# Packet sizes and store order in a transfer-bound image rotation: two slabs turned as a pair

## The chip, the cores and the metric

The kernel runs on one core of a Trainium2 chip. The metric is device time in microseconds (us).

## The reference

```python
batch, c, h, w = 32, 3, 256, 256
def reference(x):                       # float32
    return np.rot90(x, k=-1, axes=(-2, -1)).astype(np.float32)
```

96 images of 256 x 256 floats are rotated by 90 degrees. 25.17 MB are read and 25.17 MB written, and nothing is calculated.

## The kernel before

The images are cut into 12 slabs of 2 MB, eight images each. A slab is loaded into a buffer (`unit`), turned by VectorE in two transposes, and stored. All loads stand in the queue ahead of all stores. (In the cuts of code, "..." marks what is left out, and comments in English are added.) Slab n is turned into the place that slab n - 1 has left, so twelve buffers and one in PSUM are enough.

The way in which a slab lies in its buffer sets the size of the contiguous pieces ("packets") that a transfer moves. "Short" means 8 rows, 8 KB; "long" means 16 rows, 16 KB. With these turns, a slab may have long packets on one side only: long in and short out, or short in and long out.

```python
RL, RS = 16, 8
I = 2
long_st = (0, 1, 2, last)               # short loads, long stores; the others the reverse
...
for n in range(n_slabs):
    t_in, t_out = units[n], units[n - 1] if n else turned0
    if n in long_st:
        ...                             # two transposes
    else:
        src = t_in.rearrange("p i f -> p (i f)").rearrange("p (r g c) -> p c r g", r=RL, c=RS)
        dst = t_out.rearrange("p i (c k r) -> p c r k i", c=RS, r=RL)[:, :, ::-1, ::-1, :]
        for h in range(2):
            cs = slice(h * RS // 2, (h + 1) * RS // 2)
            nc.vector.transpose(out=dst[:, cs], in_=src[:, cs])
    if n in range(5, last):
        nc.sync.dma_start(out=st_short[n], in_=t_out)          # one store of 2 MB
    elif n:
        for i in range(I):
            st = store(n, t_out, i)                            # two stores of 1 MB
            ...                         # slab 1's first store is ordered after slab 11's first load
```

Slab 0 is turned into PSUM, copied back to SBUF by ScalarE at the end, and stored last.

## Time and profile before

| | before |
|---|---|
| time, median of the first 3 runs | 123.80 us (123.74 to 123.87) |
| span of the profile | 121.9 us |
| packet time, share of 16 engines' span | 98.1% |
| VectorE busy | 92.9 us (76%) |
| packets | 5248: 3072 of 8 KB, 1536 of 16 KB, 640 tiny ones for semaphores |

The lines on which the argument rests are shown in the prediction below. Two more from the profile's page: the groups of VectorE work (line, engine, operation, names, shapes, count | busy us, mean ns of one | idle time before) and the packet count.

```profile
DMA packets 5248, 50.33 MB, mean 413 GB/s; under 512 B 640, under 2 KB 640, under 8 KB 640
...
L98 DVE STREAM_TRANSPOSE u<-u 128x2048 f32<-128x2048 f32 x16 | 62.4, 3947 | 0.3
L92 DVE STREAM_TRANSPOSE u<-u 128x2048 f32<-128x2048 f32 x6 | 23.4, 3984 | 0.1
```

A transpose of 2048 columns takes 3.95 to 3.98 us, and VectorE waits for nothing in between.

### The profile page before, as it was taken

To read this page: it belongs to the slowest core of one execution; us is meant where nothing else is said; L and a number is where in the kernel's file an instruction comes from. 1 tells how busy PE (TensorE), PEld (TensorE's weight loads), DVE (VectorE), ACT (ScalarE), POOL (GpSimd) and SP (SyncE) were. 2 spreads that over 40 slices of the span, in tenths; PEclk is the share of its full clock that TensorE was granted. 3 is DMA by queue.
4 is the path that set the end of the run, shared out by engine and by line. 5 is a ranking of instruction groups with operands and counts; after the bars stand their busy time and mean duration, and the time that the engine had idled before them with its cause. 6 is when DMAs were issued, how large, how long until landed. Compare 5 with 4: busy or idle time off the path is not lost.

```text
span 121.9 us, 137 instructions
## 1 busy us (share of the span) xinstructions
DVE 92.9 (76%) x24; ACT 4.9 (4%) x3; POOL 0.2 (0%) x4
## 2 busy tenths in 40 slices
DVE  0039999999999999999999999999999992000000
ACT  0000000000000000000400000000000007400000
POOL 0000000000000000000000000000000000000000
DMA  3999999999999999999999999999999999999994
GB/s 86 430 430 430 427 433 430 430 430 430 430 430 430 430 430 430 430 430 390 427 468 430 430 390 430 430 430 430 411 419 419 427 419 419 414 427 473 425 419 188
DMA packets 5248, 50.33 MB, mean 413 GB/s; under 512 B 640, under 2 KB 640, under 8 KB 640
## 3 DMA queue, kind: packets, MB, share of 16 engines
q1 hardware_dynamic: 5248, 50.33, 98.1%
HBM read 25.17 MB, written 25.17 MB: 413 GB/s over the span
## 4 chain that ended last, share of the span: by engine, by line
DVE 44%; issue 29%; DMA 6%; DVEq 3%; ACT 2%; ACTq 1%; SPq 0%
DVE u L98 26%; DVE u L92 12%; DVE turned L92 6%; DMA u<-in_x_dram 6%; DVEq L138 3%; ACT u L110 2%; ACTq L138 1%; SPq L73 0%; DVEq L92 0%
## 5 line engine op out<-in xcount | busy, mean ns | idle before, releaser
L98 DVE STREAM_TRANSPOSE u<-u 128x2048 f32<-128x2048 f32 x16 | 62.4, 3947 | 0.3
L92 DVE STREAM_TRANSPOSE u<-u 128x2048 f32<-128x2048 f32 x6 | 23.4, 3984 | 0.1
L92 DVE STREAM_TRANSPOSE turned<-u 128x2048 f32<-128x2048 f32 x2 | 7.1, 3586 | 8.1 <-DMA u<-in_x_dram 8.1
L110 ACT COPY u<-turned 128x2048 f32<-128x2048 f32 x2 | 3.6, 1869 | 40.5 <-DVE u L92 40.5
L110 ACT ACT_TABLE_LOAD x1 | 1.3, 1283 | 59.6 <-DMA u<-in_x_dram 59.6
L127 POOL MEMSET const-bfloat16-1.0<- 128x1 bf16 x1 | 0.1, 102 | 0.0
L127 POOL MEMSET const-uint8-127<- 128x1 uint8 x1 | 0.1, 102 | 0.0
L127 POOL MEMSET const-float32-0.0<- 128x1 f32 x1 | 0.1, 99 | 0.2 <-issue 0.2
L127 POOL MEMSET const-float32-1.0<- 128x1 f32 x1 | 0.1, 99 | 0.0
## 6 DMA issues: line engine op xcount, KB each, us to landing
u<-in_x_dram SPq DMA_DIRECT2D x20, 1024.0 KB, 19.6
out_dram<-u SPq DMA_DIRECT2D x12, 1024.0 KB, 12.1
out_dram<-u SPq DMA_DIRECT2D x6, 2048.0 KB, 20.9
u<-in_x_dram SPq DMA_DIRECT2D x2, 2048.0 KB, 13.5
```

The costliest lines, as they stand in the source:

```text
L92: nc.vector.transpose(out=dst[:, cs], in_=src[:, cs])
L98: nc.vector.transpose(out=dst[:, cs], in_=src[:, cs])
L110: nc.scalar.copy(out=units[last][:, i], in_=turned0[:, i])
L127: nc = _bacc.Bacc("TRN2", target_bir_lowering=False, num_devices=1)
L138: with _tile.TileContext(nc) as tc:
```

## The change

The intent is to have long packets on more sides. Slabs 8 and 9 are turned together, as a pair: with two neighbouring buffers read as one and two neighbouring buffers written as one, both sides can be long. The place of the pair must be two free, adjacent buffers; these are those of slabs 3 and 7. Buffer 3 holds slab 4's turned data, so slab 4 must be stored before the pair is turned. That is why slab 4 is stored ahead of all; 3 and 5 to 7 follow, and 1 and 2 come behind them. Slab 10 changes from long loads and short stores to the reverse.

```diff
-    long_st = (0, 1, 2, last)
+    long_st = (0, 1, 2, 10, 11)
+    both = (8,)
+    paired = [n + a for n in both for a in range(2)]
...
+    adjacent = [(3, 7), (8, 9)]        # these share one tile
...
+    for n in (0, 1, 2, 3, 7, 4, 5, 6, *range(8, n_slabs)):      # order of the loads
...
+        elif n in paired:
+            src = pairs[both.index(n) + 1].rearrange("p a (r g c) -> p c r g a", r=RL, c=RL)
+            dst = pairs[both.index(n)].rearrange("p i (c k r) -> p c r k i", c=RL, r=RL)[:, :, ::-1, ::-1, :]
+            parts, step = 4, RL // 4
...
+    for n in range(both[0]):
+        turn(n)
+    for n in (4, 3, 5, 6, 7, 1, 2):
+        st = store(n)                  # 3 to 7 as one store of 2 MB each
+    for n in range(both[0], n_slabs):
+        turn(n)
+        store(n)
```

| | loads of 16 KB | loads of 8 KB | stores of 16 KB | stores of 8 KB | order of the stores |
|---|---|---|---|---|---|
| before | 3 to 10 | 0, 1, 2, 11 | 0, 1, 2, 11 | 3 to 10 | 1, 2, 3 ... 11, 0 |
| after | 3 to 9 | 0, 1, 2, 10, 11 | 0, 1, 2, 8 to 11 | 3 to 7 | 4, 3, 5, 6, 7, 1, 2, 8 ... 11, 0 |

More of the change, by code (lines that the diff above doesn't have):

```diff
@@ L60, with fours @@
     ld_short, ld_long, st_short, st_long = short(rows_in), long(rows_in), short(rows_out), long(rows_out)
-    pools = [ctx.enter_context(tc.tile_pool(name=f"unit{u}", bufs=1)) for u in range(n_slabs)]
-    units = [pool.tile([P, I, F], fp32, name=f"u{u}") for u, pool in enumerate(pools)]
-    psum = ctx.enter_context(tc.tile_pool(name="psum", bufs=1, space=bass.MemoryType.PSUM))
-    turned0 = psum.tile([P, I, F], fp32, name="turned0")
-    for n in range(n_slabs):
-        if n in (1, 2):
-            ld = nc.sync.dma_start(out=units[n], in_=ld_short[n])
+    units = [None] * n_slabs
+    adjacent = [(3, 7), (8, 9)]
+    pairs = []
+    for us in adjacent + [(u,) for u in range(n_slabs) if all(u not in us for us in adjacent)]:
+        pool = ctx.enter_context(tc.tile_pool(name=f"unit{us[0]}", bufs=1))
+        held = pool.tile([P, len(us), I * F], fp32, name=f"u{us[0]}")
+        for j, u in enumerate(us):
+            units[u] = held[:, j]
+        pairs.append(held)
+    psum = ctx.enter_context(tc.tile_pool(name="psum", bufs=1, space=bass.MemoryType.PSUM))
+    turned0 = psum.tile([P, I * F], fp32, name="turned0")
+    def fours(t):
+        return t.rearrange("p (i f) -> p i f", i=I)
+    for n in (0, 1, 2, 3, 7, 4, 5, 6, *range(8, n_slabs)):
+        if n in (1, 2, 10):
+            nc.sync.dma_start(out=fours(units[n]), in_=ld_short[n])
             continue
@@ L72 @@
             if n in long_st:
-                ld = nc.sync.dma_start(out=units[n][:, i], in_=ld_short[n][:, i])
+                ld = nc.sync.dma_start(out=fours(units[n])[:, i], in_=ld_short[n][:, i])
             else:
-                ld = nc.sync.dma_start(out=units[n][i::I].rearrange("p i f -> p (i f)"), in_=ld_long[n, i])
+                ld = nc.sync.dma_start(out=units[n][i::I], in_=ld_long[n, i])
             if (n, i) == (last, 0):
                 mark = ld
-    def store(n, t, i):
+    home = [turned0] + units[:last]
@@ L80, in store, with turn @@
+    def turn(n):
         if n in long_st:
-            return nc.sync.dma_start(out=st_long[n, i], in_=t[i::I].rearrange("p i f -> p (i f)"))
-        return nc.sync.dma_start(out=st_short[n][:, i], in_=t[:, i])
-    for n in range(n_slabs):
-        t_in, t_out = units[n], units[n - 1] if n else turned0
-        if n in long_st:
-            src = t_in.rearrange("p i (r g c) -> p c r g i", r=RS, c=RL)
-            dst = t_out.rearrange("p i f -> p (i f)").rearrange("p (c k r) -> p c r k", c=RL, r=RS)[:, :, ::-1, ::-1]
-            pieces = 2
-            for h in range(pieces):
-                cs = slice(h * RL // pieces, (h + 1) * RL // pieces)
-                nc.vector.transpose(out=dst[:, cs], in_=src[:, cs])
-        else:
-            src = t_in.rearrange("p i f -> p (i f)").rearrange("p (r g c) -> p c r g", r=RL, c=RS)
-            dst = t_out.rearrange("p i (c k r) -> p c r k i", c=RS, r=RL)[:, :, ::-1, ::-1, :]
-            for h in range(2):
-                cs = slice(h * RS // 2, (h + 1) * RS // 2)
-                nc.vector.transpose(out=dst[:, cs], in_=src[:, cs])
-        if n in range(5, last):
-            nc.sync.dma_start(out=st_short[n], in_=t_out)
-        elif n:
-            for i in range(I):
-                st = store(n, t_out, i)
-                if (n, i) == (1, 0):
-                    tc.add_manual_dep(st.ins, mark.ins.name, mybir.DependencyInfo(
-                        mybir.DependencyClass.Sync, mybir.DependencyReason.SCHED_ONLY), reason="stores after loads")
@@ new lines, in turn @@
+            src = fours(units[n]).rearrange("p i (r g c) -> p c r g i", r=RS, c=RL)
+            dst = home[n].rearrange("p (c k r) -> p c r k", c=RL, r=RS)[:, :, ::-1, ::-1]
+            parts, step = 2, RL // 2
+        elif n in paired:
+            if n not in both:
+                return
+            src = pairs[both.index(n) + 1].rearrange("p a (r g c) -> p c r g a", r=RL, c=RL)
+            dst = pairs[both.index(n)].rearrange("p i (c k r) -> p c r k i", c=RL, r=RL)[:, :, ::-1, ::-1, :]
+            parts, step = 4, RL // 4
+        else:
+            src = units[n].rearrange("p (r g c) -> p c r g", r=RL, c=RS)
+            dst = fours(home[n]).rearrange("p i (c k r) -> p c r k i", c=RS, r=RL)[:, :, ::-1, ::-1, :]
+            parts, step = 2, RS // 2
@@ new lines, in turn, with store @@
+        for h in range(parts):
+            nc.vector.transpose(out=dst[:, h * step : (h + 1) * step], in_=src[:, h * step : (h + 1) * step])
+    def store(n):
+        if n in paired:
+            first = n if n in both else n - 1
+            for i in range(I):
+                nc.sync.dma_start(out=st_long[n, i], in_=pairs[both.index(first)][n - first :: I, i])
+        elif n in long_st:
+            for i in range(I):
+                nc.sync.dma_start(out=st_long[n, i], in_=home[n][i::I])
+        else:
+            return nc.sync.dma_start(out=st_short[n], in_=fours(home[n]))
@@ L109 @@
+    for n in range(both[0]):
+        turn(n)
+    for n in (4, 3, 5, 6, 7, 1, 2):
+        st = store(n)
+        if n == 4:
+            tc.add_manual_dep(st.ins, mark.ins.name, mybir.DependencyInfo(
+                mybir.DependencyClass.Sync, mybir.DependencyReason.SCHED_ONLY), reason="stores after loads")
+    for n in range(both[0], n_slabs):
+        turn(n)
+        store(n)
     for i in range(I):
-        nc.scalar.copy(out=units[last][:, i], in_=turned0[:, i])
-    for i in range(I):
-        store(0, units[last], i)
+        nc.scalar.copy(out=fours(units[last])[:, i], in_=fours(turned0)[:, i])
@@ L116 @@
+    home[0] = units[last]
+    store(0)
 _INS = ['x']
```

## The prediction

> **What bounds the kernel now.** The program moves 25.17 MB in and 25.17 MB out and only rearranges in between, so I read the slices and the queue line of the page first, to see whether the transfers ever stop.
>
> ```profile
> DVE  0039999999999999999999999999999992000000
> DMA  3999999999999999999999999999999999999994
> GB/s 86 430 430 430 427 433 430 430 430 430 430 430 430 430 430 430 430 430 390 427 468 430 430 390 430 430 430 430 411 419 419 427 419 419 414 427 473 425 419 188
> ...
> q1 hardware_dynamic: 5248, 50.33, 98.1%
> ...
> DVE 44%; issue 29%; DMA 6%; DVEq 3%; ACT 2%; ACTq 1%; SPq 0%
> ```
>
> The row DMA is at 9 from the second slice to the one before the last: the 16 transfer engines are full for the whole run, at 98.1% of the span. The last line here, the chain that ended last, would name VectorE (44%) and "issue" (29%). It is to be distrusted: it follows semaphores back from the last instruction, and the last instruction is the wait for the last store. The row DVE falls to 0 six slices (18 us) before the end, while the transfers go on. VectorE keeps up, with slack; it does not set the end.
>
> The second view is busy time by stretch (start:end, length, busy time of DVE, ACT and POOL, clock, DMA share, GB/s). I cut it where the packet records change size: 8 KB loads, 16 KB loads, 16 KB stores, 8 KB stores, 16 KB stores.
>
> ```profile
> 7.30:17.20 9.90, 9.10 (x3) 0.00 (x0) 0.00 (x0) 1.00 1.00 424
> 17.20:56.30 39.10, 38.93 (x11) 0.00 (x0) 0.00 (x0) 1.00 1.01 429
> 61.30:71.00 9.70, 9.63 (x4) 0.00 (x0) 0.00 (x0) 1.00 1.01 432
> 71.00:110.70 39.70, 30.27 (x8) 3.63 (x2) 0.00 (x0) 1.00 1.01 423
> 110.70:120.50 9.80, 0.00 (x0) 0.00 (x0) 0.00 (x0) 1.00 1.01 428
> ```
>
> Share 1.00 to 1.01 everywhere: no idle transfer engine inside, loads first and then stores, one after the other. The rate is 424 to 432 GB/s whatever the packet size. All that a change of packet sizes can win lies in that small difference.
>
> The third view is the timeline from 54 us and the SyncE queue's waits, for the slack of the engines behind the transfers:
>
> ```profile
> 59.63 3.97 SPq L81 DMA_DIRECT2D out_dram<-u  x4
> 59.64 1.28 ACT L110 ACT_TABLE_LOAD   x1 [59.64 <-DMA u<-in_x_dram]
> ...
> 93.56 7.82 DVE L92 STREAM_TRANSPOSE u<-u 128x2048 f32<-128x2048 f32 x2
> 101.40 5.57 SPq L81 DMA_DIRECT2D out_dram<-u  x4
> ```
> ```profile
> SPq L81 <- DMA u<-in_x_dram: 16.8, 1, 16.8
> SPq L81 <- DVE u L92: 7.4, 1, 7.4
> ```
>
> The first store is issued at 59.63 us, held 16.8 us by the load it is ordered after. Slab 11's stores are issued at 101.40 us, right after its turn; in the packet records they only begin to move at 110.72 us. So VectorE is some 9.3 us ahead of the transfers at the end.
>
> From the packet records, each slab of 2 MB takes (sum of its packets' durations over 16 engines, in us): slab 0's load 5.37 (start-up), 8 KB loads of slabs 1, 2 and 11 4.94, 4.99 and 5.02, 16 KB loads 4.91 each; 16 KB stores 4.89 each at 61 to 71 us and 4.93 each at the end; 8 KB stores 4.95, 4.95, 4.98 and 5.01 for slabs 3 to 6, and 5.02 to 5.05 for 7 to 10. Loads 59.62, stores 59.65, together 119.27. The first packet starts at 1.76 us and the last ends at 120.77 us: that is 119.01 us, the packets overlapping a trifle. The remaining 2.9 us of the span are start-up and the last landing.
>
> **What the Trainium skill says.** "DMA: Bandwidth & Descriptors", section "Where 436 GB/s comes from": 16 ports of 32 bytes at 850 MHz, 435.2 GB/s, are the ceiling. The trace agrees: 423 to 432 GB/s is 97 to 99% of it, so no ordering can win over 3%. The same page, "Why small descriptors are slow (HBM only)": an overhead of about 3 cycles a packet beside one cycle for 32 bytes. An estimate with that page's 850 MHz clock is 3.5 ns a packet. The loads agree: two median 8 KB packets of 309 ns against one of 614 ns (mean) leave 4 ns. The late stores show more, two of 314 ns (means) against 616.6 ns: 11 ns. Measured numbers are used below. "Anatomy of one DMA — SWDGE (gpsimd) path" puts most of its 2.0 us fixed cost in the write receipt; these DMAs are issued from SyncE, not GpSimd, and the trace shows 1.16 us from the last packet's end (120.77) to the end of the span (121.93).
>
> **The change part by part.**
> Loads. Slab 10 goes from 16 KB to 8 KB packets, the other eleven keep their size (slab 7 only comes earlier). Slab 10 costs 5.0 instead of 4.91: +0.08 us. The DMAs stay 40 (22 loads + 18 stores become 21 + 19).
> Stores. Slabs 8, 9 and 10 go from 8 KB to 16 KB: three at 5.02 become three at about 4.93, -0.28 us. The five that stay 8 KB (3 to 7) move to the front, where before the first four cost 4.95 to 5.01: I take 4.97 each, 24.85, against 24.93 for the same slabs before: -0.08. Slabs 1 and 2 move back, where I take 4.91 instead of 4.89: +0.04. Slabs 11 and 0 stay last. Sum of stores -0.32.
> All packets: -0.24 us. A second way agrees: 512 packets of 8 KB become 256 of 16 KB; the overall means, 314.4 and 614.0 ns, save 14.8 ns a pair, 256 x 14.8 / 16 = 0.24 us.
> VectorE. Still 24 transposes of 2048 columns a partition. The pair's four read with a larger step, but the two forms in place now, with quite different steps, take 3947 and 3984 ns a piece, so I keep 3.95 us: no change of the 92.9 us. What moves is when the pair's outputs come free: all four pieces must be done before slab 8 or 9 can be stored, 70.0 + 4 x 3.93 = 85.8 us.
> Waits. The build's order of instructions shows the pair waiting on the store of slab 4, whose place it overwrites; that is why slab 4 is stored first. That store moves at about 61.4 to 66.4 us and has landed at some 67.6 (with the 1.16 us above); VectorE is free for the pair at 70.0 us. Hidden by 2.4 us. In the new order, slab 8's stores have their turn in the transfers at 61.4 + 7 x 4.95 = 96.1 us, 10.3 us after the pair is turned; slab 10's at 106, turned at 93.7; slab 11's at 111, turned at 101.5; slab 0's at 116, copied by ScalarE at 105. Every step stays hidden.
> The sum: 123.8 - 0.24, rounded with the changeover below to 123.6 us.
>
> **The rivals.**
> 1. A bubble at the changeover from loads to stores. The first store is now one DMA of 2 MB (issues of such stores last 1.2 us here, first issues of 1 MB 0.5 us). At the start, 1.03 us pass from the first issue to the first packet; 59.63 + 1.03 = 60.7, before the loads run dry at 61.6. If packets only start after the whole 1.2 us issue, the engines idle a few tenths of a us: 123.8 to 124.0. I put 0.1 us of it into the sum.
> 2. The pair's wait takes over. For it: four pieces in a row with one release, behind a store that has just begun. Against it: a margin of 2.4 us before VectorE waits at all, and then 8 to 10 us before the transfers feel it. It would need pieces of over 6 us: then 127 or so. Little chance.
> 3. The order, not the size, made the late 8 KB stores dear (4.95 rising to 5.05 while slabs go by): then those moved forward cost 4.95 each, or those in the late places all gain more, another -0.2: 123.3. If the drift belongs to the slab and not to the size, the gain shrinks to 0.1: 123.7.
> 4. The 16 KB stores cure more than packet durations show. They cannot: the engines have no idle time for it. Even all 24 slab transfers at 4.89 would save 119.27 - 117.4 = 1.9 us, 1.5%.
>
> **Range and chances.** Every path but 2 stays within half a per cent. Runs of the kernel before spread by 0.13 us. I predict 123.6 us, range 123.0 to 124.1, faster by over 2% 0.02, within 2% 0.96, slower by over 2% 0.02.
>
> **What would show it.** In the profile after: the queue line at about 98% with 4992 packets; the stretch of 16 KB stores at the end at 427 GB/s or above, and 8 KB stores in front; summed packet time near 119.0 us; DVE near 93 us in 24 pieces of 3.9 us without a wait before the pair over 0.5 us; no slice in the middle of the row DMA under 9. It would be wrong if that row has a hole at 61 us (rival 1), if VectorE waits for a store for many us (rival 2), or if packets of one size changed their duration by over 2%.

## The result

The changed kernel takes 123.33 us (median of 6 runs, 123.22 to 123.68) against 123.84 us (123.74 to 123.90). The ratio is 0.9964, 95% interval 0.9950 to 0.9977. Ratios here are the mean time of one kernel's fast runs over that of the other's of the same rounds, so not quite the ratio of the medians that are quoted. Measured twice more, in later rounds, the ratio was 0.9978 (0.9964 to 0.9992) and 0.9971 (0.9958 to 0.9983). The change wins 0.2 to 0.4%: 0.27 to 0.45 us of 123.8.

First, the slices and the queue line of the page after, to be held against those that the prediction shows:

```profile
DVE  0039999999999999999999999999999990000000
DMA  2999999999999999999999999999999999999994
GB/s 78 426 431 421 431 456 431 431 421 421 431 426 431 431 431 426 404 421 415 418 431 431 429 431 429 423 429 429 464 426 426 426 431 431 431 431 426 431 431 194
DMA packets 4992, 50.33 MB, mean 414 GB/s; under 512 B 640, under 2 KB 640, under 8 KB 640
q1 hardware_dynamic: 4992, 50.33, 97.9%
```

The transfers still never stop, the packets are the 4992 that were expected, and the mean rate went from 413 to 414 GB/s. There is no hole in the middle of the row DMA, where the loads give way to the stores.

Second, busy time by stretch (start:end, length, busy time of DVE, ACT and POOL with counts, clock, DMA share, GB/s), cut where the packet size changes: 8 KB loads, 16 KB loads, 8 KB loads, 8 KB stores, 16 KB stores.

```profile
7.40:17.20 9.80, 8.99 (x3) 0.00 (x0) 0.00 (x0) 1.00 1.01 425
17.20:51.50 34.30, 34.16 (x10) 0.00 (x0) 0.00 (x0) 1.00 1.01 429
51.50:61.40 9.90, 9.87 (x3) 1.28 (x1) 0.00 (x0) 1.00 1.00 419
61.50:86.00 24.50, 24.40 (x8) 0.00 (x0) 0.00 (x0) 1.00 1.01 429
86.00:120.10 34.10, 14.20 (x4) 3.63 (x2) 0.00 (x0) 1.00 1.01 429
```

The stretch of 8 KB stores is the one to look at. Before it ran at 423 GB/s (71.00 to 110.70 us, in the prediction). Now it runs at 429, as fast as 16 KB packets. Where a stretch is cut shifts such a rate by a few GB/s, so this is a hint and no more; the table below has the times.

Third, VectorE after, in the groups of the page and in the timeline (start us, us, engine, line, operation, names, count).

```profile
L116 DVE STREAM_TRANSPOSE u<-u 128x2048 f32<-128x2048 f32 x22 | 84.6, 3912 | 0.3
```
```profile
15.29 84.94 DVE L116 STREAM_TRANSPOSE u<-u 128x2048 f32<-128x2048 f32 x22
...
84.56 4.76 SPq L122 DMA_DIRECT2D out_dram<-u  x4
92.41 13.42 SPq L125 DMA_DIRECT2D out_dram<-u  x6
```

The 22 transposes follow one another from 15.29 us with 0.3 us of idle time in sum: VectorE didn't wait for the pair's place. The pair was done at 84.56 us, when its stores were issued; in the packet records they begin to move at 95.68 us, 11.1 us later. The pair stays hidden.

The gain is too small for whole views, so I take it from the packet records, slab by slab. There are two measures. One is the prediction's: durations of a slab's packets, summed over 16 engines. The other is by the clock: the mean end of a slab's last 16 packets less that of the slab before. Packet records overlap a little, so the second is 0.02 to 0.05 us smaller for most slabs, and only the second adds up to the time that passed.

| stretch (us) | predicted change | summed durations, before to after | by the clock, before to after |
|---|---|---|---|
| load of slab 0 (with the start-up) | 0 | 5.37 to 5.18 | 7.46 to 7.56 |
| load of slab 10 | +0.08 | 4.91 to 5.02 | 4.89 to 4.97 |
| the other ten loads | 0 | 49.33 to 49.32 | 49.07 to 49.06 |
| stores of 3 to 7 (8 KB, moved to the front) | -0.08 | 24.93 to 24.73 | 24.72 to 24.51 |
| stores of 8 to 10 (8 KB to 16 KB) | -0.28 | 15.07 to 14.71 | 14.93 to 14.65 |
| stores of 1 and 2 (moved back) | +0.04 | 9.78 to 9.78 | 9.74 to 9.74 |
| stores of 11 and 0 | 0 | 9.87 to 9.82 | 9.83 to 9.79 |

By the clock the stores win 0.54 us (59.23 to 58.69), and the loads lose 0.17, of which 0.08 is slab 10. The rest, 0.10 in slab 0's load, is start-up; it was 7.48 and 7.45 us in the other two profiles of the same kernel, so it is chance. The last packet ends at 120.37 us instead of 120.77.

The records show one thing more. A packet that nothing disturbs takes 309 ns (8 KB) or 611 ns (16 KB), to the nanosecond. In the profile before, the 8 KB stores ran so until 79 us; from there to the end most took 312 to 319 ns. After the change, hardly one packet between 63 and 93 us is longer than that floor.

### The profile page after: what moved, and what is told of

Same layout as the page of the kernel before. It is cut to its first block, busy times and chain, and to the rows that moved or that the text cites. A ratio compares the mean times of both kernels' runs of the same rounds, so it can differ in the third digit from the quotient of the medians.

```text
span 121.5 us, 135 instructions
## 1 busy us (share of the span) xinstructions
DVE 91.7 (75%) x24; ACT 4.9 (4%) x3; POOL 0.2 (0%) x4
## 2 busy tenths in 40 slices
DMA packets 4992, 50.33 MB, mean 414 GB/s; under 512 B 640, under 2 KB 640, under 8 KB 640
## 3 DMA queue, kind: packets, MB, share of 16 engines
q1 hardware_dynamic: 4992, 50.33, 97.9%
## 4 chain that ended last, share of the span: by engine, by line
DVE 56%; issue 17%; DMA 6%; DVEq 3%; ACT 2%; ACTq 1%; SPq 0%
DVE u L116 50%; DVE turned L116 6%; DMA u<-in_x_dram 6%; DVEq L169 3%; ACT u L141 2%; ACTq L169 1%; SPq L92 0%; DVEq L116 0%
## 5 line engine op out<-in xcount | busy, mean ns | idle before, releaser
L116 DVE STREAM_TRANSPOSE u<-u 128x2048 f32<-128x2048 f32 x22 | 84.6, 3912 | 0.3
```

The source lines that it names most:

```text
L116: nc.vector.transpose(out=dst[:, h * step : (h + 1) * step], in_=src[:, h * step : (h + 1) * step])
```

## The experiments

Two theories. **P:** the gain is the packet sizes: fewer packets, each with its fixed cost. **O:** a good part is the order: the five slabs that stay at 8 KB are stored in an undisturbed stretch, where 8 KB packets are nearly as good as 16 KB ones. Each run below gave the right output.

**after_again: the changed kernel once more.** No edit.

> The changed kernel once more, on this chip, as the mark for the other three. Both theories: about 123.3 us, ratio to before 0.996. Its packet times should again show clean stretches (8 KB stores at 309 ns, 16 KB at 611 ns) in the front part of the stores. If the late point at which packets get longer (93.8 us in the first profile) moves about from run to run, that point is chance and part of the gain is luck; if it stays, something in the program sets it.

Measured: 123.51 us (123.31 to 123.71), ratio 0.9978. The profile has the same clean front; this time packets get longer from 78 us on, not from 94. So when the disturbance starts moves about in this kernel, while the floor stays. By the mark set above, that point is chance, and a small part of the first profile's gain is luck: by the clock the stores take 58.69, 58.74 and, in after_third, 58.77 us.

**order_only: the sizes of before in the order of after.**

```diff
+    for n in (4, 3, 5, 6, 7, 1, 2, 8, 9, 10, last):
+        ...                     # two long stores of 1 MB, or one short one of 2 MB
```

> Packet sizes, loads and buffers of before; only the order of the stores is that of the change (4, 3, 5, 6, 7, 1, 2, then 8, 9, 10, 11, 0), 5248 packets. Theory P (the gain is the 256 saved packets alone): nothing gained, 123.8 us, ratio 1.000. Theory O (the gain is largely that the 8 KB stores come in a stretch where packets run undisturbed): slabs 3 to 7 take 24.73 us instead of 24.93, so 123.6 us, ratio 0.998; slabs 8 to 10 stay at 5.02 each. If both act, O's number here and about 123.5 in size_only.

The edit does one thing more: slabs 3 and 4 go out as one store of 2 MB each, as in the change, where the kernel before has two of 1 MB. So there are 5216 packets, not 5248.

Measured: 123.71 us (123.61 to 124.00), ratio 0.9995 (0.9982 to 1.0007): no difference that the runs can tell. The profile shows what the order does. The stretches are 8 KB stores (3 to 7), 16 KB stores (1, 2), 8 KB stores (8 to 10); the last, of 16 KB stores, is left out:

```profile
61.30:85.80 24.50, 24.40 (x7) 0.00 (x0) 0.00 (x0) 1.00 1.01 429
85.80:95.50 9.70, 9.63 (x4) 0.00 (x0) 0.00 (x0) 1.00 1.00 428
95.50:110.45 14.95, 6.04 (x2) 3.63 (x2) 0.00 (x0) 1.00 1.01 421
```

Slabs 3 to 7 run at 429 GB/s and take 24.53 us, as in the change. Slabs 8 to 10, still 8 KB, run at 421 GB/s and take 14.88 us. The profiled run was also the quickest of the five, 123.61 us. So O's effect is visible in one profile (0.19 us in slabs 3 to 7), but the order alone is not shown to make the kernel faster.

**size_only: the sizes and the pair of after, with slabs 1 and 2 stored first again.**

```diff
-    for n in (4, 3, 5, 6, 7, 1, 2):
+    for n in (1, 2, 4, 3, 5, 6, 7):
```

> Pair, packet sizes and loads of the change, 4992 packets; the stores of slabs 1 and 2 come first again, as before (1, 2, 4, 3, 5, 6, 7, then 8 to 11, 0). Theory P: slabs 8 to 10 take 14.71 us instead of 15.07 and everything else is as in the change, 123.3 to 123.4 us, ratio 0.996 to 0.997. Theory O: most of the gain is lost, 123.6 to 123.8. VectorE should now wait some 7 us before the pair, since slab 4's store lands at about 77.3 us instead of 67.6; the pair is done at about 92 us and its stores have their turn at 96, so that wait should cost nothing.

Measured: 123.45 us (123.36 to 123.47), ratio 0.9967 (0.9955 to 0.9980), beside 0.9978 of the change in the same rounds. The gain stays without the new place of slabs 1 and 2. By the stretches (16 KB stores, 8 KB stores, 16 KB stores) and the wait:

```profile
61.40:71.10 9.70, 8.72 (x3) 0.00 (x0) 0.00 (x0) 1.00 1.02 437
71.10:95.70 24.60, 18.58 (x6) 0.00 (x0) 0.00 (x0) 1.00 1.01 426
95.70:119.90 24.20, 11.45 (x3) 3.63 (x2) 0.00 (x0) 1.00 1.02 434
```
```profile
DVE u L116 <- issue: 6.9, 1, 6.9
```

Cuts at slab borders shift these rates by a few GB/s, so I use the records: the 8 KB stores of slabs 3 to 7, now from 71 to 96 us, still take 24.52 us, and almost no packet is longer than its floor up to the end. Theory O said that a late place makes 8 KB packets dear. It falls: the same places that cost up to 5.00 us a slab before cost 4.90 to 4.92 here. But P does not account for the whole gain either. By the clock the stores of 8 to 10, whose packets grew, win 0.34 us here (14.93 to 14.59), and those of 3 to 7, whose packets did not, win 0.20 (24.72 to 24.52). VectorE waited 6.9 us for the pair's place (the view names no releaser; slab 4's last packet ended at 76.45 us, and VectorE started at 77.08). It cost nothing, as worked out.

**unpaired: slabs 8 and 9 treated as 10 and 11 are, without the pair.**

```diff
-    long_st = (0, 1, 2, 10, 11)
-    both = (8,)
+    long_st = (0, 1, 2, 8, 9, 10, 11)
+    both = ()
```

> The change without its pair: slabs 8 and 9 are loaded in 8 KB packets and turned one by one, as 10 and 11 are; all stores as in the change. 5248 packets less 128 x 2 on the store side and more on the load side. Theory P: two 8 KB loads at 5.02 us instead of 4.91, 0.2 us above the change, 123.5 us. If the pair in itself costs or wins by when it releases its stores: a difference other than 0.1 to 0.3.

Measured: 123.60 us (123.51 to 123.96), ratio 0.9985 (0.9972 to 0.9997), against 0.9978 of the change beside it. The loads of slabs 8 to 11 run at

```profile
41.40:61.40 20.00, 19.93 (x6) 1.28 (x1) 0.00 (x0) 1.00 1.00 417
```

where the change, with 16 KB loads for 8 and 9, has

```profile
41.70:61.40 19.70, 19.63 (x6) 1.28 (x1) 0.00 (x0) 1.00 1.01 424
```

The two loads cost 9.94 us instead of 9.79 by the clock. The pair is worth these 0.15 us in the profile. The times, 0.09 us apart, cannot settle it: their intervals overlap.

Held against order_only, this run gives the cleanest test of P: the order of the stores and the number of packets (5216) are the same, and slabs 8 to 10 are stored in packets of 16 KB instead of 8 (with loads and turns to match). By the clock those three stores take 14.66 us instead of 14.88, and slabs 3 to 7 take 24.56 and 24.53. What is won on the stores is lost again on the loads of 8 to 10, now short. The other profiles agree: slabs 8 to 10 take 14.88 to 14.95 us in the four where they are stored in 8 KB packets, and 14.59 to 14.70 in the eight with 16 KB packets and no gap.

**half_packets: the kernel before, with the stores of slabs 5 to 10 in 4 KB packets.**

```diff
-            nc.sync.dma_start(out=st_short[n], in_=t_out)
+            for k in range(2):
+                ks = slice(k * F // 2, (k + 1) * F // 2)
+                nc.sync.dma_start(out=st_short[n][:, :, ks], in_=t_out[:, :, ks])
```

> The kernel before with the stores of slabs 5 to 10 in 4 KB packets instead of 8 KB (two column halves for each, 1536 packets more, 6784 in all). If a packet costs the 3.5 ns[...] (and that the undisturbed stretches show: 4.90 against 4.87 us a slab for 128 packets more), 1536 x 3.5 / 16 = 0.34 us more: 124.2 us. If it costs the 11 ns that the late stores of before showed, 1.06 us more: 124.9 us.

Measured: 125.72 us (125.68 to 125.81), ratio 1.0158 (1.0142 to 1.0173), slower by 2.0 us: more than either number expected. (The packets are 6880, not the 6784 that I had counted: six more stores bring 96 tiny semaphore packets.) The stretch of slabs 3 and 4, left at 8 KB, and that of the 4 KB stores:

```profile
71.00:80.80 9.80, 9.77 (x3) 0.00 (x0) 0.00 (x0) 1.00 1.01 425
80.80:112.00 31.20, 20.57 (x6) 3.63 (x2) 0.00 (x0) 1.00 1.02 398
```

The six slabs take 31.61 us instead of 29.83 by the clock. 1.78 us x 16 engines over 1536 more packets is 18.5 ns for each packet more. In the records the undisturbed floor of a 4 KB packet is 159 ns, and two of them make 318 ns, 9 ns more than one of 8 KB; their mean is 167.5 ns. So smaller packets do cost time, and in a disturbed stretch a packet costs more than at its floor. That is P, with a cost that is not constant.

**pair_late: slab 4 stored last of the seven.**

```diff
-    for n in (4, 3, 5, 6, 7, 1, 2):
+    for n in (3, 5, 6, 7, 1, 2, 4):
```

> The change, but slab 4, whose store frees the pair's place, is stored last of the seven (3, 5, 6, 7, 1, 2, 4). Sizes and counts are the same, so a theory of packet sizes alone says 123.5 us. The reading of the waits says: slab 4's store lands at about 97 us instead of 67.6, VectorE then needs 14.7 us for the pair's four pieces, slab 8's stores begin at about 113 us instead of 95.7, the transfer engines idle for 17 us, and the time is 140 to 142 us. This is rival 2 of the prediction made to happen.

Measured: 140.78 us (two runs), ratio 1.1374 (1.1353 to 1.1395). From the slices, the wait and the stretch of the gap:

```profile
DVE  0069999999999999999910000001999999994000
...
DMA  4999999999999999999999999995000079998995
```
```profile
DVE u L116 <- DMA out_dram<-u: 26.5, 1, 26.5
```
```profile
96.00:112.20 16.20, 15.47 (x5) 0.00 (x0) 0.00 (x0) 1.00 0.00 0
```

VectorE waits 26.5 us for the store of slab 4, and then the transfers stand still for 16.2 us while the pair is turned. This is rival 2 of the prediction made to happen. Same packets, same sizes, 14% slower: the place of slab 4 in the order is what keeps the pair's wait hidden; it is not what wins the 0.3%.

**before_again: the kernel before, profiled a second time.** No edit.

> The kernel before, for a second profile. In the first one, the 8 KB stores ran at 309 ns up to 79 us and then, from about 1 us after a 2 MB store was issued at 77.9 us, at 312 to 316 ns to the end; larger disturbances followed the issues at 85.7 and 93.6 us. If the program sets this, the second profile shows the same three places; if it is chance, they lie elsewhere. Time 123.8 us either way.

Measured: 123.93 us. Packets held up by 45 to 58 ns lie at 79, 87 and 95 us again, about 1 us after the stores issued at 78.0, 85.8 and 93.7 us; a further one lies at 72 to 74 us. The excess over the floor, summed over the packets of one microsecond, is 94, 421 and 650 ns at 79, 87 and 94 us in the first profile, and 283, 563 and 437 ns in the second, where the next microsecond has 602 ns. So in this kernel the places come back, and something in the program has a part in where packets are held up.

**split_stores: the stores of slabs 5 to 10 as two of 1 MB, against the suspicion that the 2 MB issues disturb.**

```diff
-        if n in range(5, last):
+        if n in range(5, 5):
```

> The kernel before with the stores of slabs 5 to 10 as two DMAs of 1 MB each, as those of 3 and 4 already are, instead of one of 2 MB; packets stay 8 KB, the order stays. Both profiles of before show packets held up by 30 to 58 ns about 1 us after the 2 MB stores issued at 77.9, 85.8 and 93.6 us, and longer packets from then on. Theory H (those 2 MB issues set the disturbance, and the change gains partly because its late stores are 1 MB): slabs 5 to 10 fall from 4.93 to 5.01 us by the clock of the packets to about 4.91, some 0.3 us less, 123.5 us. If the disturbance has another cause: 123.8 us, as before, and slabs 7 to 10 stay near 4.98.

Measured: 123.90 us, ratio 1.0017 (1.0004 to 1.0029). Slabs 8 to 10 take 14.95 us by the clock, as before. Theory H falls. Only the size of the issues is ruled out, though, not the issues as such. In after_third, too, the excess has peaks (53, 126 and 175 ns summed over one microsecond, at 85, 93 and 101 us) about 1 us after stores are issued (84.66, 92.51 and 100.36 us); but size_only issues stores at 91.50, 99.36 and 107.21 us and shows none. So an issue alone is not enough.

A rival stands untested. Slabs 3 to 7 take 24.72, 24.81 and 24.75 us in the three profiles with the order of before, and 24.51 to 24.56 in all ten with any of the changed orders, order_only among them. All ten also store slabs 3 and 4 as one store of 2 MB each instead of two of 1 MB, and no run tests that alone. What sets the disturbance, and why the stores after the change meet less of it, stays open.

**two_pairs, two_pairs_again, two_pairs_long_first: the change carried on.** Slabs 10 and 11 become a second pair, turned into the place of 8 and 9; the third of these kernels also stores 1 and 2 directly behind 4.

```diff
-    long_st = (0, 1, 2, 10, 11)
-    both = (8,)
-    adjacent = [(3, 7), (8, 9)]
+    long_st = (0, 1, 2)
+    both = (8, 10)
+    adjacent = [(3, 7), (8, 9), (10, 11)]
```

> The change carried on: slabs 10 and 11 become a second pair, turned into the place that slabs 8 and 9 left, so that all loads but those of slabs 0 to 2 and all stores but those of 3 to 7 have 16 KB packets (4736 in all, 256 fewer than the change). Theory P (packet size sets the pace): two loads at 4.90 us instead of 4.97 by the clock of the packets, 0.14 us less than the change, 123.2 to 123.4 us, ratio 0.996. Rival W (the second pair's four pieces in a row hold back slab 10's stores): they are turned at about 100.3 us and have their turn at 105.4, a margin of 5 us, so a gap in the transfers and a time above 123.6 would speak for it.

> The changed kernel a third time, beside its successors on the same chip. The two measurements so far gave ratios of 0.9964 and 0.9978; 123.3 to 123.5 us.

> The kernel with two pairs again, for a comparison on one chip with the change. Theory P: 0.1 us below the change, 123.25 to 123.4. If it is not below, the second pair's saving of two short loads (0.14 us) is lost again to longer packets in its stores, as its first profile shows (12 slabs of stores in 58.87 us, 58.69 in the change).

> Two pairs, with the 16 KB stores of slabs 1 and 2 right behind slab 4's (4, 1, 2, 3, 5, 6, 7), as in size_only, whose stores were undisturbed to the end. Slab 4 is still first, so VectorE does not wait for the pair's place. If the order makes the stretch undisturbed, stores take 58.6 us instead of 58.87: 123.1 us, the fastest of all. If that was chance: 123.3 us.

Measured: two_pairs 123.33 us, ratio 0.9964 (0.9952 to 0.9977). Then on one chip: the change (after_third) 123.33 us, 0.9971 (0.9958 to 0.9983); two_pairs_again 123.33 us, 0.9968 (0.9956 to 0.9981); two_pairs_long_first 123.28 us (123.16 to 123.36), 0.9961 (0.9947 to 0.9975). There are 4752 packets (my 4736 left out the semaphores of one more load). The loads of 10 and 11 fall from 9.94 to 9.79 us, as expected. The last of these kernels has the lowest time of all and beats the kernel before, but whether it beats the change lies within the intervals: 0.05 us in the median. Its stores take 58.70 us, not the 58.6 expected, with packets over the floor from 92 us on: by its own mark, that size_only was undisturbed to the end was chance and not the order. None is a gap in the transfers, so rival W is not seen.

## Why the prediction was right

The prediction said 123.6 us, within 2%; it came to 123.33, inside the range of 123.0 to 124.1. Part of the agreement is easy: a range of 1.1 us is wide beside a gain of 0.27 to 0.45 us. Its steps:

- **The bound.** Right. Transfer share 97.9% after; VectorE lost 1.2 us of busy time (92.9 to 91.7) and that changed nothing. The chain of waits, which named VectorE before, names it with 56% after: still not the bound. The prediction's reason, that the transfers go on after VectorE has stopped, holds in both profiles. pair_late shows the other side: put off VectorE by 26.5 us, more than its margin, and the end moves by 17 us.
- **Loads.** "Slab 10 costs 5.0 instead of 4.91": it cost 5.02. Right.
- **Stores of slabs 8 to 10.** Predicted -0.28; -0.36 in the same measure, and -0.28 by the clock. Right: unpaired against order_only shows 0.22 us from the packet size of these stores, with order and packet count the same.
- **Stores of slabs 3 to 7.** This is the term that was mis-sized. "The first four cost 4.95 to 5.01: I take 4.97 each", a gain of 0.08; they cost 4.95 each and gained 0.20. The prediction took the drift of 8 KB stores (4.95 to 5.05) as something that stays in its place. Rival 3 had the other reading, that the order made them dear. Neither is quite it. In size_only 8 KB stores in the late places stay at their floor, so the place is not the cause; in order_only the earlier places are clean without any change of size. The cost comes with a disturbance which the programs meet at different times, and whose cause I could not name: split_stores ruled out the size of the store issues. (Slabs 1 and 2 were to lose 0.04 by moving back; they lost nothing.)
- **VectorE.** "I keep 3.95 us" was wrong for the pair: its four pieces took 3.67 to 3.68 us. Off the path, it changed only the margin.
- **Waits.** Right to about a microsecond: pair ready at 85.8 us predicted and 84.56 measured, its stores' turn at 96.1 and 95.68. The 1.16 us taken for the landing of slab 4's store was too long: pair_late has 0.64 us from its last packet (96.06) to the start of the pair (96.70).
- **Rivals.** No bubble at the changeover (rival 1: the first store moves at 61.47 us, just as the loads end). Rival 4's bound, 1.5% even if every slab were at its best, still stands: none of the kernels tried won more than 0.4%.
- **The sum.** 123.8 - 0.24 + 0.1 for the changeover is 123.66, so 123.7 and not 123.6; the 0.1 never came.
- **A reading.** "Two median 8 KB packets of 309 ns against one of 614 ns (mean)" holds a median against a mean. The two floors, 2 x 309 against 611, leave 7 ns by the records' durations, and 3.8 by the clock (last section).
- **Two ways to the same sum.** The prediction's two estimates of -0.24 agreed partly by luck: the second used the mean of all 8 KB packets, those of the start-up (slab 0, mean 336 ns) among them. Without slab 0 the mean is 312.2 ns and the saving 0.17 us. And both were sums of packet durations, and these overlap. Measured in that way the change is -0.70 us, of which 0.19 is start-up that did not shorten the run; by the clock of the last packet it is -0.40, and by the runs -0.27 to -0.45.

## What to carry to other kernels

When the transfer engines are busy over 98% of the span, ask first how far the rate is from its best stretch; here that bounded any gain at 1.5%, and a change with many parts won 0.3%. Doubling the packet size paid less here where packets were larger: by the clock, a step from 8 to 4 KB cost 0.30 us a slab (1.78 over six), and one from 8 to 16 KB won 0.09 (0.28 over three). Not all that a change wins need come from the part that was meant to win it: here 0.20 us fell to slabs whose packets stayed as they were. A turn that needs someone's place to be free is free of cost as long as its wait stays inside the margin of the engine, so put that store first, and work out the margin from the issue of a store and the time when its packets move.

## What the Trainium skill lacked or had wrong

- "DMA: Bandwidth & Descriptors", section "Why small descriptors are slow (HBM only)", gives about 3 cycles a packet (3.5 ns as an estimate with that page's clock). Undisturbed stretches agree: 4.90 against 4.87 us a slab for 128 packets more is 3.8 ns. What it lacks is that the cost is not constant: late 8 KB stores took 4.98 us a slab before against 4.89 for 16 KB ones in the change, 11 ns a packet, and in half_packets each of the 1536 packets that came with the halving cost 18.5 ns.
- No page says that 16 engines can fall out of an undisturbed state, in which nearly every 8 KB packet takes 309 ns and nearly every 16 KB packet 611 ns, and stay out of it for tens of microseconds, with most packets at 312 to 319 and 613 to 629 ns.
- "VectorE: DVE Perf Modes", section "The three transpose paths", has one figure for the VectorE transpose, a 128 x 128 bf16 block, and that section has nothing on float32 and access patterns. Here the same 128 x 2048 float32 transpose took 3.95 to 3.98 us in two patterns and 3.67 us in the pair's (3.59 us where it wrote to PSUM, in the pattern that took 3.98 into SBUF).
- "DMA: Bandwidth & Descriptors", section "Anatomy of one DMA — SWDGE (gpsimd) path", covers stores issued from GpSimd. For one issued from SyncE, size_only and pair_late show 0.63 and 0.64 us from the last packet of a store to the start of the VectorE work that waited for it.
